# One pool of 19 slots for raw and split weight tiles, and the last tokens of a feed-forward stage ended one by one

## The chip, the core and the metric

The kernel runs on one core of a Trainium2 chip. Its engines each run their own list of instructions in order, and wait for each other by semaphores: TensorE (PE, matmuls into PSUM), VectorE (DVE), ScalarE (ACT), GpSimd (POOL) and SyncE (SP, which here only issues the DMAs). The metric is the device time of one execution in microseconds (us), lower is better.

## The reference

A decoder trunk of two layers on 512 tokens of width 1024, all in float32:

```
def reference(x, ...):
    for i in range(DEPTH):                       # 2 layers
        h = rmsnorm(x, norm_mix_pre[i])
        if i % N_MIXERS == 0:
            m = swa_sink_attention(h, ...)       # 16 heads of 64, 4 kv heads, window 128
        else:
            m = chunked_sgu(h, ...)              # gelu, layernorm, 128x128 mixing per chunk
        x = x + rmsnorm(m, norm_mix_post[i])
        h = rmsnorm(x, norm_ffn_pre[i])
        x = x + rmsnorm(swiglu(h, ffn_w_gate_up[i], ffn_w_down[i]), norm_ffn_post[i])
    return x                                     # FF = 2816
```

## The kernel before

The 512 tokens are four tiles of 128 (tokens 0 to 3 below are these tiles), 1024 is eight k-tiles of 128, and 2816 is 22. A float32 product is made of three: a value is split into a high part (`hh` for activations, `wh` for weights) and a low part (`hl`, `wl`), and `mm3` adds hh·wh, hl·wh and hh·wl in PSUM, each matmul in the helper at L272. So every weight is loaded and split before PE uses it.

Weights come in chunks of eight 128x128 blocks (128x1024 float32, 512 KB). `fetch` (L303) has SP issue the DMA into a tile `raw`; `split` has ACT copy raw to `wh` (L344), and DVE subtract, raw - wh, to `wl` (L325; POOL at L322 for the first two chunks). In parts of the feed-forward stages a chunk is the sum or difference of two raws (DVE at L337, then ACT at L332). Before, raws have a pool of their own with 4 buffers (`rawp`), and wh, wl, the gain rows and attention's values share 15 slots of 128x1024 (`wp`).

The stages are numbered 0 (Q, K, V and attention), 1 (its out-projection), 2 (first feed-forward, gate and up, and most of the down-projection), 3 (the end of its down-projection), 4 and 5 (SGU, out-projection), and 6 and 7 (second feed-forward). In stage 3 and 7 the last six k-tiles (BJ = 6) of the down-projection are added token by token and in two halves of 512 columns: the loop over `ends`. Each entry names tokens and a half; 6 k-tiles x 3 matmuls per token and half run on PE, and DVE adds the PSUM result to `m` (L901).

When both halves of a token are there, `Tok` ends it: ACT squares and sums (L476), DVE or POOL multiplies by the gain row (L604, L598), DVE computes a reciprocal root of the mean square in eight small rows (L482 and L455 to L471), and updates x in two halves (L617). When tokens 0 and 1 (or 2 and 3) are updated, `NextH` norms the pair for the next stage: the same small rows for both, a scaling (L523 on DVE, L520 on ACT), transposes on PE into `aux` (L554), and the copies `hh` (ACT, L567) and `hl` (DVE, L571) of two k-tiles at a time, which the first matmuls of the next stage read. `LastTok` is the last token of the program, cut in 256-column halves (L930, L651, L662).

In attention, ACT makes the softmax p (L1070) and scales it (L1083), PE transposes it into aux (L1116), ACT copies that to `t` (L1120), and PE multiplies t with the values vt (L1108); ACT copies the result to `ga` (L1130) and DVE makes its low part (L1135). Beside it runs the rotation of the next heads (ACT `rt`, L966; `ga<-rt`, L976).

The order of all this is set while the program is built, by a planner in the kernel: `now` is its estimate of PE's time, `busy` that of the other engines. Work beside the main matmuls is held in generators (`Side`) with due times, and `tick`, `until` and `wait` run them when they are due. `split_idle` splits the next chunk early when engines are idle or the chunk is urgent, by the numbers of `PLAN` for the stage, `pace` and `hold` (a time before which the next chunk isn't needed). `used` and `raw_used` count slots that are taken in the plan; `cur` is the chunk that PE is at. A change in any of these moves instructions on several engines.

Of the kernel before, what the change touches and what calls it, by code (L numbers as in the profile page):

```python
# [6 lines left out]
F32 = mybir.dt.float32  # L7
# [6 lines left out]
P = 128  # L14
# [7 lines left out]
CB = 8  # L22
NEG = -1.0e30
MAGIC = 0x5F3759DF
NW = 15
NP = 2
PITCH = 0.107
NY = 3
P0 = 3
NT = 3  # L30
NRAW = 4
SETS = (8, 8)
AJ = sum(SETS)
BJ = NJ - AJ
# [60 lines left out]
def _stream():  # L95

    st, n = [], [0]

    def plain(blocks, uses):
        for _ in range(blocks // CB):  # L100
            st.append(((n[0],), 0, uses))
            n[0] += 1

    def ffn():
        plain(3 * 2 * KT, 2)
        plain((SETS[0] - 3) * 2 * KT, 1)
        gb = n[0]
        qb = gb + 2 * (NJ - SETS[0])
        for kind, a, b in ITEMS:
            if kind == "g":  # L110
                st.append(((gb + 2 * (a - SETS[0]) + b,), 0, 1))
            else:
                x, y, sign = PRODUCTS[a[1]][1]
                at = lambda z: qb + 4 * b + 2 * z[0] + z[1]
                st.append(((at(x),) if y is None else (at(x), at(y)), sign, 2))
        n[0] = qb + 4 * NQ
        plain(2 * BJ * 4, 4)

    plain(16, 4)
    plain(80, 1)  # L120
    plain(64, 4)
    ffn()
    plain(32, 4)
    plain(16, 2)
    plain(32, 4)
    plain(48, 1)
    plain(64, 4)
    ffn()
    return st, n[0]


STREAM, NHBM = _stream()
# [17 lines left out]
def trunk_kernel(ctx, tc, x_t, xt, w, cols, rows, ws_t, consts, out):  # L150
    nc = tc.nc
    pool = lambda n, b, **k: ctx.enter_context(tc.tile_pool(name=n, bufs=b, **k))
# [2 lines left out]
    hp = pool("hp", KT)  # L155
    mp = pool("mp", 2 * NB)
    gp = pool("gp", 2)
    rawp = pool("rawp", NRAW)
    wp = pool("wp", NW)
    tp = pool("tp", 3)  # L160
    sp = pool("sp", 3)
# [5 lines left out]
    def nm(s):  # L167
        cnt[0] += 1
        return f"{s}_{cnt[0]}"
# [26 lines left out]
    now = [0.0]  # L196
# [23 lines left out]
    def first():  # L220
        return min(sides, key=lambda s: s.due)

    def tick():
        while True:
            if sides and first().due <= now[0]:
                first().step()
            elif not split_idle():
                return
# [21 lines left out]
    def until(f):  # L250
        while not f():
            tick()
            if not f():
                pass_time(max(now[0] + 0.01, first().due))
# [29 lines left out]
    NCH = NBLK // CB  # L284
    raws, chunks = {}, {}
    used, cur, hold, pace = [0], [0], [0.0], [5.1]
    left = [CB * u for _, _, u in STREAM]
    raw_used = [0]

    def fetch(free=0.0, most=NBLK):  # L290
        while len(raws) < min(NCH, most) and raw_used[0] + len(STREAM[len(raws)][0]) <= NRAW:
            c = len(raws)
            if c == NLATE:
                load_x()
            if c == NLATE + 1:
                nc.sync.dma_start(c_msk[:, 0:256], consts[:, 1024:1280])
                nc.sync.dma_start(c_msk[:, 256:384], consts[:, 1408:1536])
                nc.sync.dma_start(cs[:], consts[:, 0:1024])
                busy["d"] += 2.5
            tiles = []  # L300
            for b in reversed(STREAM[c][0]):
                raw = rawp.tile([P, CB * P], F32, tag="raw", name=nm("raw"))
                nc.sync.dma_start(raw[:], w[b])  # L303
                busy["d"] = max(busy["d"], now[0], free) + 1.46
                tiles.insert(0, raw)
            raw_used[0] += len(tiles)
            raws[c] = (tiles, busy["d"] + DLAT)

    def split():
        c = len(chunks)  # L310
        fetch()
        tiles, ready = raws[c]
        raw = tiles[0]
        assert used[0] + 2 <= NW
        used[0] += 2
        wh = wp.tile([P, CB * P], F32R, tag="w", name=nm("wh"))
        wl = wp.tile([P, CB * P], F32R, tag="w", name=nm("wl"))

        def low(f):
            yield f  # L320
            if c in POOL_LOW:
                nc.gpsimd.tensor_tensor(wl[:], raw[:], wh[:].bitcast(F32), ALU.subtract)  # L322
                chunks[c][3] = f + 2.4
            else:
                nc.vector.tensor_tensor(wl[:], raw[:], wh[:].bitcast(F32), ALU.subtract)  # L325
                chunks[c][3] = V(CB * P, f)
            raw_used[0] -= 1
            fetch(chunks[c][3])

        def high_low(f):  # L330
            yield f
            nc.scalar.activation(wh[:], raw[:], AF.Copy)  # L332
            yield from low(A(CB * P, f))

        if len(tiles) == 2:
            op = ALU.add if STREAM[c][1] > 0 else ALU.subtract
            nc.vector.tensor_tensor(raw[:], raw[:], tiles[1][:], op)  # L337
            f = V(CB * P, ready)
            raw_used[0] -= 1
            fetch(f)  # L340
            chunks[c] = [wh, wl, None, None, f]
            chunks[c][2] = Side(high_low(f), f)
            return
        nc.scalar.activation(wh[:], raw[:], AF.Copy)  # L344
        f = A(CB * P, ready)
        chunks[c] = [wh, wl, None, None, f]
        chunks[c][2] = Side(low(f), f)

    def split_idle():
        c = len(chunks)  # L350
        if c >= NCH or used[0] + 2 + spare[0] > NW or (c and not chunks[c - 1][2].done):
            return False
        if c not in raws or raws[c][1] > now[0]:
            return False
        slack = max(now[0], hold[0]) + (c - cur[0] - 1) * pace[0] - max(now[0], busy["v"], busy["a"]) - (2.4 if len(STREAM[c][0]) == 1 else 3.7)
        urgent, idle, ahead = PLAN[stage[0]][:3]
        if slack > urgent:
            if max(busy["v"], busy["a"]) > now[0] + idle or any(s.chain and s.due < now[0] + ahead for s in sides):
                return False
        split()  # L360
        return True

    spare, stage = [0], [0]

    def chunk(i):
        c = i // CB
        while c >= len(chunks):
            until(lambda: not chunks or chunks[len(chunks) - 1][2].done)
            split()
        return c, chunks[c]  # L370

    def high(i, n):
# [15 lines left out]
        return ch[0][:, o:o + w], ch[1][:, o:o + w]  # L388

    def row_tile(o):  # L390
        used[0] += 1
        assert used[0] <= NW
        t = wp.tile([P, D], F32, tag="w", name=nm("row"))
        nc.sync.dma_start(t[:], rows[272 + o * D:272 + (o + 1) * D].partition_broadcast(P))
        return t
# [308 lines left out]
    def ffn(base, nx_in, g1o, nx_out):  # L704
# [186 lines left out]
        d0 = at  # L891
        l = gsrc(g)
        if 1:
            spare[0] = 0
            g1 = row_tile(g1o)
            toks = [Tok(t, m[t], g1, nx_out) for t in range(NB)]
            if nx_out is None:
                toks[-1] = LastTok(NB - 1, m[-1], g1, m[0])

            def add(t, c, ps):  # L900
                nc.vector.tensor_tensor(m[t][c][:], ps[:], m[t][c][:], ALU.add)  # L901
                toks[t].add(c, ps, V(S, now[0] + 0.2))

            ends = [(0, 0), (0, 1), (1, 0), (1, 1)]
            if nx_out is None:
                ends.pop()
            ends = [((0, 1), 0), ((0, 1), 1)] + [((2 + i,), c) for i, c in ends]
            for n, (ts, c) in enumerate(ends):
                if n == 2:
                    hold[0] = now[0] + 4 * BJ * 0.65  # L910
                for t in ts:
                    grab("acc")
                ps = [acc() for _ in ts]
                for k in range(BJ):
                    for t, q in zip(ts, ps):
                        tok_mm(q, l, t, k, d0 + c * BJ * 4 + 4 * k, k == 0, k == BJ - 1)
                for t, q in zip(ts, ps):
                    add(t, c, q)
            if nx_out is None:
                t = NB - 1  # L920
                until(lambda: toks[0].done)
                for i, hf in enumerate(halves):
                    grab("acc")
                    ps = acc()[:, 0:256]
                    for k in range(BJ):
                        lh, ll = l(k, slice(t * P, (t + 1) * P))
                        wh, wl = blk(d0 + BJ * 4 + 4 * k, 4 if i else 0, 4)
                        mm3(ps, lh, ll, wh[:, hf], wl[:, hf], k == 0, k == BJ - 1)
                        tick()
                    nc.vector.tensor_tensor(m[t][1][:, hf], ps, m[t][1][:, hf], ALU.add)  # L930
                    toks[t].add(i + 1, ps, V(256, now[0] + 0.2))
            else:
                drop_after(toks)
# [613 lines left out]
```

## Time and profile before

| | before |
|---|---|
| median of 3 runs | 1058.82 us (1058.65 to 1059.26) |
| the profiled execution | 1059.33 us, span 1057.5 us |
| PE busy | 1031.1 us (97%), mean granted clock 0.989 |
| PE weight loads busy | 854.7 us (81%) |
| DVE busy | 684.7 us (65%) |
| ACT busy | 469.6 us (44%) |
| POOL busy | 23.8 us (2%) |
| raw DMAs | 240 of 512 KB, 3.6 us from issue to landing (median) |

Busy time is the time in which an engine had an instruction of its own running. In a row of a timeline the first number is the start in us from the span's start, the second the time it took (several equal rows together as xN), then engine, line, operation and output<-inputs; in brackets stands how long the engine idled before it, and the instruction that released it. In a row of a table of stretches stand the length, the busy time and count of PE, PEld, DVE, ACT and POOL, the granted clock of PE, the share of the DMA engines and GB/s. Groups by line show busy time and the mean in ns of one.

### The profile page before, as it was taken

To read this page: it belongs to the slowest core of one execution; us is meant where nothing else is said; L and a number is where in the kernel's file an instruction comes from. 1 tells how busy PE (TensorE), PEld (TensorE's weight loads), DVE (VectorE), ACT (ScalarE), POOL (GpSimd) and SP (SyncE) were. 2 spreads that over 40 slices of the span, in tenths; PEclk is the share of its full clock that TensorE was granted. 3 is DMA by queue.
4 is the path that set the end of the run, shared out by engine and by line. 5 is a ranking of instruction groups with operands and counts; after the bars stand their busy time and mean duration, and the time that the engine had idled before them with its cause. 6 is when DMAs were issued, how large, how long until landed. Compare 5 with 4: busy or idle time off the path is not lost.

```text
span 1057.5 us, 13471 instructions
## 1 busy us (share of the span) xinstructions
PE 1031.1 (97%) x5126; PEld 854.7 (81%) x5126; DVE 684.7 (65%) x1276; ACT 469.6 (44%) x817; POOL 23.8 (2%) x22
## 2 busy tenths in 40 slices
PE   8998998999999999999989999999999999999996
PEld 7875665998888888888878888899888888888885
DVE  6798678743446566778495777474245666687736
ACT  5798666542233343435265343464224333334411
POOL 2000002000000000000010000010000000000000
PEclk9998999999999999999999999999999999999999
DMA  9422011343425644655431333133344553565402
GB/s 334 138 82 80 21 60 41 100 127 113 139 82 178 199 122 157 222 188 191 156 116 60 104 103 121 56 121 120 120 140 131 178 174 124 188 203 193 163 21 80
DMA packets 39057, 138.66 MB, mean 131 GB/s; under 512 B 4368, under 2 KB 4896, under 8 KB 38992
## 3 DMA queue, kind: packets, MB, share of 16 engines
q1 hardware_dynamic: 38304, 136.66, 39.3%
q8 instruction: 40, 0.66, 0.3%
q10 hardware_dynamic: 576, 0.92, 0.2%
q0 software_dynamic: 112, 0.23, 0.2%
q14 instruction: 25, 0.20, 0.1%
HBM read 135.69 MB, written 2.10 MB: 130 GB/s over the span
## 4 chain that ended last, share of the span: by engine, by line
PE 92%; DVE 3%; ACT 2%; issue 1%; DMA 0%; POOL 0%; DVEq 0%; ACTq 0%; POOLq 0%
PE acc L272 89%; PE acc L1108 1%; PE aux L1116 1%; PE aux L554 1%; ACT p L1070 1%; DMA c_cols<-cols 0%; ACT rt L966 0%; DVE wl L325 0%; DVE x L617 0%; DVE hl L1393 0%; ACT wh L344 0%; PE aux L552 0%; ACT t L1120 0%; DVE m L1210 0%; DVE rc L471 0%
## 5 line engine op out<-in xcount | busy, mean ns | idle before, releaser
L272 PE MATMUL acc<-hh,wh 128*128 128x512 f32 (+1 forms) x960 | 352.1, 367 | 0.0
L272 PE MATMUL acc<-hl,wh 128*128 128x512 f32 (+1 forms) x960 | 349.9, 364 | 0.0
L272 PE MATMUL acc<-hh,wl 128*128 128x512 f32 (+1 forms) x960 | 349.7, 364 | 0.0
L325 DVE TENSOR_TENSOR wl<-raw,wh 128x1024 fp32r<-128x1024 f32 x198 | 241.9, 1230 | 151.1 <-PE acc L272 78.2
L272 PEld LDWEIGHTS acc<-hh,wh 128*128 128x128 f32 x960 | 181.1, 189 | 29.4 <-issue 0.2
L272 PEld LDWEIGHTS acc<-hh,wl 128*128 128x128 f32 x960 | 181.1, 189 | 28.7
L272 PEld LDWEIGHTS acc<-hl,wh 128*128 128x128 f32 x960 | 181.1, 189 | 28.6 <-issue 0.2
L344 ACT ACTIVATE wh<-raw 128x1024 fp32r<-128x1024 f32 x160 | 165.6, 1052 | 55.0 <-PE acc L272 48.3
L272 PE MATMUL acc<-wh,rt 128*128 128x512 f32 x496 | 162.3, 389 | 0.0
L272 PE MATMUL acc<-wh,ga 128*128 128x512 f32 (+1 forms) x344 | 120.3, 399 | 3.6 <-DVE ga L1135 2.9
L272 PEld LDWEIGHTS acc<-wh,rt 128*128 128x128 f32 x496 | 93.1, 188 | 19.4
L272 PE MATMUL acc<-wl,rt 128*128 128x512 f32 x248 | 96.5, 389 | 0.0
L272 PEld LDWEIGHTS acc<-wh,ga 128*128 128x128 f32 x344 | 65.2, 191 | 21.1 <-DVE ga L1135 3.8
L853 DVE TENSOR_TENSOR m<-m,acc 128x512 f32<-128x512 f32 x80 | 51.8, 684 | 44.2 <-PE acc L272 33.0
L272 PE MATMUL acc<-wl,ga 128*128 128x512 f32 (+1 forms) x206 | 80.0, 388 | 0.0
L332 ACT ACTIVATE wh<-raw 128x1024 fp32r<-128x1024 f32 x40 | 42.3, 1059 | 71.0 <-DVE raw L337 71.0
L831 ACT ACTIVATE rt<-t 128x512 fp32r<-128x512 f32 x40 | 25.3, 633 | 87.1 <-DVE t L826 68.7
L740 ACT ACTIVATE t<-acc 128x512 f32<-128x512 f32 (+1 forms) x38 | 20.1, 529 | 95.0 <-PE acc L272 95.0
L272 PEld LDWEIGHTS acc<-wl,rt 128*128 128x128 f32 x248 | 46.6, 188 | 9.6
L337 DVE TENSOR_TENSOR raw<-raw,raw 128x1024 f32<-128x1024 f32 x40 | 48.8, 1219 | 0.0
L272 PEld LDWEIGHTS acc<-wl,ga 128*128 128x128 f32 x206 | 39.3, 191 | 6.6
L598 POOL TENSOR_TENSOR m<-m,row 128x512 f32<-128x512 f32 x12 | 16.8, 1407 | 1012.1 <-ACT acc L476 1012.1
(135 smaller groups left out, 990.5 us busy)
## 6 DMA issues: line engine op xcount, KB each, us to landing
raw<-w SPq DMA_DIRECT2D x240, 512.0 KB, 3.6
row<-rows SPq DMA_DIRECT2D x8, 512.0 KB, 5.2
xg<-xt SPq DMA_DIRECT2D x4, 512.0 KB, 7.1
x<-x_t SPq DMA_DIRECT2D x4, 512.0 KB, 11.9
out<-x SPq DMA_DIRECT2D x4, 256.0 KB, 2.1
out<-x ACTq DMA_DIRECT2D x3, 256.0 KB, 2.1
cs<-consts SPq DMA_DIRECT2D x1, 512.0 KB, 8.3
t<-ws_t SPq DMA_DIRECT2D x2, 256.0 KB, 5.9
```

Of the source, the lines that this page charges most:

```text
L272: nc.tensor.matmul(ps, a, b, start=start, stop=stop)
L325: nc.vector.tensor_tensor(wl[:], raw[:], wh[:].bitcast(F32), ALU.subtract)
L332: nc.scalar.activation(wh[:], raw[:], AF.Copy)
L337: nc.vector.tensor_tensor(raw[:], raw[:], tiles[1][:], op)
L344: nc.scalar.activation(wh[:], raw[:], AF.Copy)
L554: nc.tensor.transpose(dst, self.src[t][k // 4][:, (k % 4) * P:(k % 4 + 1) * P], ident)
L598: nc.gpsimd.tensor_tensor(self.m[c][:], self.m[c][:], self.g1[:, cols2[c]], ALU.mult)
L740: nc.scalar.activation(t1[:, hf], pg[:, hf], AF.Silu)
L831: nc.scalar.activation(hi, src, AF.Copy)
L853: nc.vector.tensor_tensor(d, d, ps[i][:], ALU.subtract if sign == "-" else ALU.add)
L1070: nc.scalar.activation(p(j), p(j), AF.Exp, bias=st[:, j:j + 1], accum_out=sm[:, j:j + 1])
L1108: nc.tensor.matmul(po[i * 64:i * 64 + 64, :], vt[n - nkt + 1 + kt][:, o:o + 64], todo[2 * kt + i], start=kt == 0, stop=kt == nkt - 1)
```

## The change

There is one pool of 19 slots now, for raw, wh, wl and rows. At most 4 raws are held in stages 2 and 6 and at most 2 elsewhere, and a raw, a split, or a row is planned only when the sum of all taken slots stays within 19. `row_tile` waits for a slot in the plan where it asserted one; `chunk` waits until the raw is there and two slots are free (`room`); `split` calls `fetch` no more. The variable `spare`, always 0, is gone. In `ends`, tokens 0 and 1 still take their first half together, but end the second one after the other; `hold` counts five entries instead of four.

```
-NW = 15
+NW = 19
-NRAW = 4
+NRAW = (2, 4)
...
-    rawp = pool("rawp", NRAW)
...
+    stage = [0]
     def fetch(free=0.0, most=NBLK):
-        while len(raws) < min(NCH, most) and raw_used[0] + len(STREAM[len(raws)][0]) <= NRAW:
+        while len(raws) < min(NCH, most):
             c = len(raws)
+            n = len(STREAM[c][0])
+            if raw_used[0] + n > NRAW[stage[0] in (2, 6)] or used[0] + raw_used[0] + n > NW:
+                return
...
-                raw = rawp.tile([P, CB * P], F32, tag="raw", name=nm("raw"))
+                raw = wp.tile([P, CB * P], F32, tag="w", name=nm("raw"))
...
     def split():
         c = len(chunks)
-        fetch()
         tiles, ready = raws[c]
         raw = tiles[0]
-        assert used[0] + 2 <= NW
+        assert used[0] + raw_used[0] + 2 <= NW
...
     def split_idle():
         c = len(chunks)
-        if c >= NCH or used[0] + 2 + spare[0] > NW or (c and not chunks[c - 1][2].done):
+        if c >= NCH or used[0] + raw_used[0] + 2 > NW or (c and not chunks[c - 1][2].done):
             return False
...
-    spare, stage = [0], [0]
+    def room():
+        fetch()
+        return len(chunks) in raws and used[0] + raw_used[0] + 2 <= NW

     def chunk(i):
         c = i // CB
         while c >= len(chunks):
-            until(lambda: not chunks or chunks[len(chunks) - 1][2].done)
-            split()
+            until(lambda: c < len(chunks) or (not chunks or chunks[len(chunks) - 1][2].done) and room())
+            if c >= len(chunks):
+                split()
...
     def row_tile(o):
+        until(lambda: used[0] + raw_used[0] < NW)
         used[0] += 1
-        assert used[0] <= NW
...
-            ends = [(0, 0), (0, 1), (1, 0), (1, 1)]
+            ends = [((0, 1), 0), ((0,), 1), ((1,), 1), ((2,), 0), ((2,), 1), ((3,), 0), ((3,), 1)]
             if nx_out is None:
                 ends.pop()
-            ends = [((0, 1), 0), ((0, 1), 1)] + [((2 + i,), c) for i, c in ends]
             for n, (ts, c) in enumerate(ends):
                 if n == 2:
-                    hold[0] = now[0] + 4 * BJ * 0.65
+                    hold[0] = now[0] + 5 * BJ * 0.65
```

In the rows that follow, the first word is the line, which is 4 to 6 higher in the changed kernel from `split` on, and the numbers behind names differ between the two programs for the same tile.

On DVE, at the end of the first feed-forward stage (stage 3), before: m_2822 and m_2823 are the halves of token 0, m_2824 and m_2825 those of token 1, u the start of token 0's root.

```order
L901 TENSOR_TENSOR m_2822<-acc_4485,m_2822 128x512
L901 TENSOR_TENSOR m_2824<-acc_4486,m_2824 128x512
L604 TENSOR_TENSOR m_2822<-m_2822,row_4479 128x512
L604 TENSOR_TENSOR m_2824<-m_2824,row_4479 128x512
L901 TENSOR_TENSOR m_2823<-acc_4528,m_2823 128x512
L901 TENSOR_TENSOR m_2825<-acc_4529,m_2825 128x512
L604 TENSOR_TENSOR m_2823<-m_2823,row_4479 128x512
L604 TENSOR_TENSOR m_2825<-m_2825,row_4479 128x512
L482 SCALAR_TENSOR_TENSOR u_4589<-sq_4481 128x1
```

The same place after: m_2828 and m_2829 are token 0, m_2830 and m_2831 token 1.

```order
L906 TENSOR_TENSOR m_2828<-acc_4482,m_2828 128x512
L906 TENSOR_TENSOR m_2830<-acc_4483,m_2830 128x512
L610 TENSOR_TENSOR m_2828<-m_2828,row_4476 128x512
L610 TENSOR_TENSOR m_2830<-m_2830,row_4476 128x512
L906 TENSOR_TENSOR m_2829<-acc_4523,m_2829 128x512
L610 TENSOR_TENSOR m_2829<-m_2829,row_4476 128x512
L488 SCALAR_TENSOR_TENSOR u_4559<-sq_4478 128x1
```

Token 1's second add and gain no longer stand ahead of token 0's root; they come behind token 0's update of x. The transposes of the pair (four rows of aux) and the matmuls around them on PE move too: before they stand in the second half of token 3 (acc_4717), after in its first half (acc_4687).

On ACT, in attention, before: aux_1057 is a transposed p, and PE's next matmul with the values waits for t_1062.

```order
L976 ACTIVATE ga_117<-rt_830 128x512
L1083 ACTIVATE p_863<-p_863,sm_862 128x256
L344 ACTIVATE wh_1038<-raw_757 128x1024
L966 ACTIVATE rt_1010<-rt_1010,c_cols 32x512 x4
L1083 ACTIVATE p_863<-p_863,sm_862 128x256
L1120 ACTIVATE t_1062<-aux_1057 128x512
L976 ACTIVATE ga_117<-rt_915 128x512
```

After, where that copy is t_1039 and the chunk's high part wh_1042:

```order
L980 ACTIVATE ga_114<-rt_823 128x512
L970 ACTIVATE rt_905<-rt_905,c_cols 32x512 x4
L1124 ACTIVATE t_1001<-aux_996 128x512
L1087 ACTIVATE p_853<-p_853,sm_852 128x256
L1124 ACTIVATE t_1039<-aux_1034 128x512
L1087 ACTIVATE p_853<-p_853,sm_852 128x256
L346 ACTIVATE wh_1042<-raw_936 128x1024
L970 ACTIVATE rt_1003<-rt_1003,c_cols 32x512 x4
L1134 ACTIVATE ga_114<-acc_967 128x4x128
```

The copy stands ahead of the chunk's high part and of the four rt now; the four rt of the heads before (rt_905) have moved in front of the copy t_1001.

Some heads later on ACT, before:

```order
L1083 ACTIVATE p_1461<-p_1461,sm_1460 128x256
L1067 ACTIVATE es_1459<-es_1459 128x4
L1070 ACTIVATE p_1461,sm_1460<-p_1461,st_1458 128x256 x4
L476 ACTIVATE acc_1500,sq_1499<-m_1011 128x512
L344 ACTIVATE wh_1584<-raw_997 128x1024
L1120 ACTIVATE t_1592<-aux_1587 128x512
```

and after:

```order
L1087 ACTIVATE p_1454<-p_1454,sm_1453 128x256
L1071 ACTIVATE es_1452<-es_1452 128x4
L1074 ACTIVATE p_1454,sm_1453<-p_1454,st_1451 128x256 x4
L1124 ACTIVATE t_1577<-aux_1572 128x512
L482 ACTIVATE acc_1493,sq_1492<-m_1004 128x512
L346 ACTIVATE wh_1584<-raw_1264 128x1024
```

The copy t has passed a square (L476, now L482) and the high part of a chunk.

More of the change, by code (lines that the diff above doesn't have):

```diff
@@ L893, in ffn @@
         if 1:
-            spare[0] = 0
             g1 = row_tile(g1o)
```

## The prediction

> **What bounds the kernel now.** I read the chain that ended last first, then the waits of TensorE (PE), then a table of stretches by time, and last the timelines of the engines around each wait.
>
> ```profile
> PE 92%; DVE 3%; ACT 2%; issue 1%; DMA 0%; POOL 0%; DVEq 0%; ACTq 0%; POOLq 0%
> ...
> PE acc L1108 <- ACT t L1120: 6.6, 3, 3.8
> ...
> PE acc L272 <- DVE ga L1135: 2.9, 2, 2.6
> PE acc L272 <- DVE hl L571: 2.7, 1, 2.7
> ...
> PE acc L272 <- DVE hl L1393: 0.8, 1, 0.8
> ...
> 92.00:106.00 14.00, 9.94 (x39) 4.84 (x38) 10.28 (x26) 10.23 (x18) 0.00 (x0) 0.76 0.23 75
> ...
> 146.00:156.00 10.00, 7.42 (x35) 4.24 (x34) 6.11 (x20) 6.67 (x19) 0.00 (x0) 0.84 0.16 51
> ...
> 176.00:187.00 11.00, 7.71 (x24) 4.59 (x23) 10.74 (x36) 5.96 (x14) 2.80 (x2) 0.84 0.30 96
> 187.00:512.00 325.00, 325.00 (x1596) 275.96 (x1595) 198.56 (x266) 125.98 (x173) 0.00 (x0) 1.00 0.48 156
> ...
> 548.00:556.00 8.00, 5.32 (x18) 3.81 (x17) 7.91 (x14) 4.66 (x11) 0.00 (x0) 0.79 0.83 294
> ```
>
> The chain is PE for 92%: the kernel is bound by its matmuls, whose number the change leaves alone. From 187 to 512 us (the first feed-forward stage) PE is busy for all 325.00 us at full clock: there is nothing to gain there, however early weights come. What can be gained is PE's waits and the slow clock behind them. The waits that this change can touch are three in attention (two for ACT's copy t, up to 3.8 us, one for DVE's ga, 2.6) and one of 2.7 us for DVE's hl, where the first feed-forward stage hands over to the SGU. In each of the four stretches with such a wait the granted clock (the last column but two) falls below 1. Length times missing clock, 14 x 0.24 = 3.4, 10 x 0.16 = 1.6, 11 x 0.16 = 1.8 and 8 x 0.21 = 1.7 us, bounds from above what the slow clock costs there; part of it falls into the waits themselves.
>
> **The change, part by part.** No instruction is added and none goes; what changes is who waits behind whom.
>
> *The end of the first feed-forward stage.* PE's rows at the hand-over:
>
> ```profile
> 547.77 0.40 PE L272 MATMUL acc<-wh,hh 128*128 128x512 f32 x1
> 548.00 0.39 PE L272 MATMUL acc<-wl,hh 128*128 128x512 f32 x1
> 551.07 0.50 PE L272 MATMUL acc<-wh,hl 128*128 128x512 f32 x1 [2.68 <-DVE hl L571]
> ...
> 553.65 0.63 PE L272 MATMUL acc<-wl,hh 128*128 128x512 f32 x1
> 554.07 0.63 PE L272 MATMUL acc<-wh,hl 128*128 128x512 f32 x1
> ```
>
> A matmul starts every 0.23 us before the wait and every 0.42 after it; the wait costs 2.7 us and the slow clock behind it up to the 1.7 above, 4.4 together. DVE before it:
>
> ```profile
> 528.20 1.37 DVE L901 TENSOR_TENSOR m<-acc,m 128x512 f32<-128x512 f32 x2 [5.30 <-PE acc L272]
> ...
> 534.74 1.41 DVE L617 SCALAR_TENSOR_TENSOR x<-m,rc,x 128x512 f32<-128x512 f32 x2
> ...
> 537.04 0.69 DVE L901 TENSOR_TENSOR m<-acc,m 128x512 f32<-128x512 f32 x1 [0.29 <-PE acc L272]
> ...
> 540.18 0.89 DVE L523 TENSOR_SCALAR m<-x,rc 128x512 f32<-128x512 f32 x2
> 541.12 0.69 DVE L901 TENSOR_TENSOR m<-acc,m 128x512 f32<-128x512 f32 x1
> ...
> 549.40 1.21 DVE L325 TENSOR_TENSOR wl<-raw,wh 128x1024 fp32r<-128x1024 f32 x1
> 550.54 0.87 DVE L571 SCALAR_TENSOR_TENSOR hl<-aux,c_cols,hh 128x256 fp32r<-128x256 f32 x2
> ```
>
> One token's half takes PE 541.12 - 537.04 = 4.08 us. Before, tokens 0 and 1 end their second half together, so DVE idles for 5.30 us up to 528.20 and then has both tokens' adds, gains, norms and updates in one pile, the last ended at 536.15; the norm of the pair and the scaling follow (540.18), then the transposes on PE and the hl that PE waits for (550.54), which by then stands behind token 2's update and wl of chunk 88. After, token 0 ends 4.08 us earlier, at about 524.6, and its gain, norm and update (some 4 us: add 0.69, a gain of as much, the small rows of the norm 1.2, the update 1.41) fit into the idle 5.30 us. Token 1's add is at 528.7, and what was two tokens' work behind it is one's: its update ends near 532.7 instead of 536.15, and the scaling comes some 3.2 us earlier. The transposes stand three chunks earlier in PE's order, so the hl of k-tiles 2 and 3 falls near 546.5 (estimate, from these rows shifted), ahead of PE's need at 548.4. Late next are wl of chunk 89 (about 550.5, needed about 550.3) and hl 4, 5 (548.6, needed 548.9): I leave 0.3 us of wait. **Term: -4.1**, between -4.4 and 0 (if the next wait takes all of it).
>
> *Attention, order alone.* The shared pool lets the planner split a chunk at other moments, and ACT's and DVE's rows move past each other. First wait, ACT:
>
> ```profile
> 94.04 0.49 ACT L1083 ACTIVATE p<-p,sm 128x256 f32<-128x256 f32 x1
> 94.44 1.04 ACT L344 ACTIVATE wh<-raw 128x1024 fp32r<-128x1024 f32 x1
> 95.51 2.91 ACT L966 ACTIVATE rt<-rt,c_cols 32x512 f32<-32x512 f32 x4
> ...
> 98.86 0.58 ACT L1120 ACTIVATE t<-aux 128x512 f32<-128x512 f32 x1
> ```
>
> The copy t for which PE stands still reads the transposes of an earlier p, but stands behind wh of chunk 16 and four rt, 1.04 + 2.91 us, and a second p. In the new order it comes ahead of these; the earlier four rt now stand ahead of the t before it. ACT would then end the two copies near 94.5 and 95.4, and PE, which has six matmuls moved up between, would be there near 92.9: waits of about 1.6 + 0.4 instead of 3.8 + 0.3, -2.1. What it passes, wh and rt, is due later: PE's next copy then falls near 100.2, as PE comes for it. Second wait:
>
> ```profile
> 149.61 0.58 ACT L476 ACTIVATE acc<-m 128x512 f32<-128x512 f32 x1
> ...
> 150.22 1.04 ACT L344 ACTIVATE wh<-raw 128x1024 fp32r<-128x1024 f32 x1
> 151.17 0.57 ACT L1120 ACTIVATE t<-aux 128x512 f32<-128x512 f32 x1
> ```
>
> PE waits 2.6 us for this t (the three waits of the row above are 6.6 in all, the largest 3.8 and a small one 0.3). It now goes ahead of a square and wh of chunk 19: 151.17 - 149.61 = 1.56 us earlier on ACT, and six matmuls move ahead of PE's wait, which cover some of it but come out of its later cover: -1.4. Third wait, DVE:
>
> ```profile
> 178.07 2.43 DVE L617 SCALAR_TENSOR_TENSOR x<-m,rc,x 128x512 f32<-128x512 f32 x2
> 180.42 1.21 DVE L325 TENSOR_TENSOR wl<-raw,wh 128x1024 fp32r<-128x1024 f32 x1
> 181.56 0.68 DVE L1210 TENSOR_TENSOR m<-acc,m 128x512 f32<-128x512 f32 x1
> 182.16 0.68 DVE L1135 TENSOR_TENSOR ga<-acc,ga 128x512 fp32r<-128x512 f32 x1
> ```
>
> The ga goes ahead of an m (0.6 us on DVE), and six matmuls (6 x 0.23 = 1.4 us) move in front of PE's wait of 2.6: -1.8. Together -5.3. Of this I give 2.0 back to waits that come next: 0.9 where PE needs p scaled for the next transposes in the second place, 0.7 at the third, 0.4 at the first. The slow clock of these three places costs at most 3.4 + 1.6 + 1.8 = 6.8 us; I take 2.0, since waits of 1 to 2 us remain, and no wait of that length stands in an attention row of before. **Term: -5.3**, between -12.1 (all waits and all slow clock) and +2 (new waits as large as the old and one more slow stretch).
>
> On the slow clock, the page "TensorE: Matmul & The Clock Gate" of the Trainium skill (section "What's actually happening") says that the clock is halved after an idle window of about 3.4 us, which runs free of the program. By it only the wait of 3.8 us would be certain to be followed by a slow stretch, and the 1.7 us at the hand-over would not hang on its wait; the sum by it would be 1.4 us smaller there. The trace differs: the wait of 2.68 us above is followed by matmuls at 0.42 us.
>
> *The end.* DVE's rows, and PE's last:
>
> ```profile
> 1049.30 0.28 PE L272 MATMUL acc<-wh,gb 128*128 128x256 f32 x1
> ...
> 1048.75 1.41 DVE L617 SCALAR_TENSOR_TENSOR x<-m,rc,x 128x512 f32<-128x512 f32 x2
> 1050.08 0.75 DVE L930 TENSOR_TENSOR m<-acc,m 128x256 f32<-128x256 f32 x2
> ...
> 1051.68 0.16 DVE L482 SCALAR_TENSOR_TENSOR u<-sq 128x1 f32<-128x1 f32 x1
> ```
>
> The same split of tokens 0 and 1 stands in the last stage. Before, token 2's update holds DVE until 1050.16, while PE's last matmul ends at 1049.6; the two adds of token 3 wait. After, the update stands ahead of token 3's work, and the last add can start with PE's end: add and gain of 0.37 each and a square of 0.58 on ACT give a u near 1050.75. **Term: -0.9**, between -1.1 and 0.
>
> *At nothing.* Raws come from the 19 slots. From the fifth on they no longer wait at the head for the reader of an earlier raw, and so land earlier, while PE still waits for ACT and for data that stand ahead of them in the same SP queue. The limit of two raws outside stages 2 and 6 is covered by this group's price and the chunk's time:
>
> ```profile
> L325 DVE TENSOR_TENSOR wl<-raw,wh 128x1024 fp32r<-128x1024 f32 x198 | 241.9, 1230 | 151.1 <-PE acc L272 78.2
> ...
> L332 ACT ACTIVATE wh<-raw 128x1024 fp32r<-128x1024 f32 x40 | 42.3, 1059 | 71.0 <-DVE raw L337 71.0
> ...
> raw<-w SPq DMA_DIRECT2D x240, 512.0 KB, 3.6
> ```
>
> From issue to usable a chunk takes 3.6 + 1.06 + 1.23 = 5.9 us, and 1.2 more for a pair (7.1); a chunk lasts PE 1057.5 / 200 = 5.3 us on the mean, so two chunks ahead (10.6 us) suffice. On SP a row now goes ahead of raw 18, 21 and 110 and three rows ahead of raw 91, and a ws_t goes behind raw 89; each of these raws is one to three transfers later (raw 91 waits for its slot anyway). A waiting raw holds every DMA behind it: raw 90 now waits for a slot until about 540.6 (it was issued at 516.4 before), raw 91 and 92 until 545.4 and 546.9; landing takes 3.6, and PE comes to chunk 90 at about 557. The wait of row_tile falls where slots are free, and the hold of 5 instead of 4 halves shifts only the planner's clock. If that cover goes, the price is that of the last rival.
>
> **The sum.** -4.1 - 5.3 - 0.9 = -10.3, from the profiled execution's 1059.33 (span 1057.5): 1049.0. That execution lies 0.5 above the median of the runs shown, so the forecast on the median is **1048.5**.
>
> **Rivals.** *Only the ends gain.* In attention ACT's work is the same and only queues up elsewhere: ACT was 10.23 of 14 us busy at the first wait, so wh and rt put back could become the next wait of the same length. For it: the window's row; against it: ACT's slack behind. It gives 1058.8 - 5.0 = 1053.8.
>
> *All goes and nothing comes back.* 4.4 + 5.3 + 6.8 + 0.9 = 17.4 less: 1041.4. Against it: three places have to fall below the wait that slows the clock, which lies between the 0.8 us of hl L1393, with matmuls at full speed behind it, and 2.6.
>
> *Shorter waits slow the clock all the same.* The waits of 1 to 2 us that I leave in attention are spread over more places; were each still followed by a stretch like 1.6 to 3.4, the clock would give nothing and PE would save 3.3 there: 1058.8 - 4.1 - 3.3 - 0.9 = 1050.5. The same page of the Trainium skill (section "A second HAM failure mode: psum-queue depth-cycling") tells of such short idling that keeps the clock swinging; no run here shows it yet.
>
> *Nothing is gained.* Chunk 87 can't be split before a slot pair comes free, in either order; if its wl now stops DVE ahead of the hl, the 2.7 us of the hand-over come back under another name, and with attention as in the first rival only the end is left: 1057.9.
>
> *Slower.* A raw that waits for the last matmul on a slot blocks SP's queue, and the chunks behind are late. A pair takes 7.1 us from issue, a chunk lasts 5.3, so a pair issued one chunk ahead is 1.8 us late. Ten of the 40 pairs late give 18 us: 1048.5 + 18 = 1066.5. It decides from seven pairs (12.4 us, the gain and the 0.2%). Against it: stages 2 and 6 keep four raws and thus the 15 slots they had.
>
> **How the numbers follow.** Forecast 0.45, with the clock rival (0.10) inside its own range 1045.5 to 1052; ends alone 0.20; all goes 0.10; nothing 0.08; slower 0.07. What a measurement tells from no change is 0.2%, 2.1 us (1056.7 to 1060.9). The range goes from 1043.5 to 1056.5: it takes in the forecast, the clock rival, most of the ends alone and the near side of "all goes". Faster 0.85, same 0.08, slower 0.07.
>
> **What would show it.** In the profile of the changed kernel: the wait for hl L571 (now L577) gone or under 1 us and a clock of 1.00 from 548 to 556; token 0's update done before token 1's add; waits for t under 2 us at the two places in attention, with a clock above 0.9 in the first stretch; the last u<-sq 1.2 us after PE's last matmul instead of 2.1. Wrong would be: waits of PE for wl or wh in stages 2 or 6, SP's raws issued behind PE's need, or a new wait of over 2.5 us between 95 and 187.

## The result, and the profile after

The changed kernel takes 1044.41 us (median of 4, 1042.74 to 1044.54), against 1059.04 for the kernel before: a ratio of 0.9858, with a 95% interval of 0.9841 to 0.9875. That is 14.6 us less; the forecast was 1048.5, 10.3 less, with a range of 1043.5 to 1056.5 that holds the result. The profiled execution took 1044.39 us, its span is 1042.6.

The waits of PE in the changed kernel (total, times, longest, in us; the lines of the two programs differ by a few, L271 is L272 of before, L346 is L344, L1124 is L1120):

```profile
PE aux L1120 <- ACT t L1124: 3.6, 3, 2.4
PE acc L271 <- ACT wh L346: 3.1, 1, 3.1
PE acc L271 <- DVE ga L1139: 2.7, 1, 2.7
```

Gone are the three waits for t ahead of the matmuls with the values (6.6 us) and the one for hl at the hand-over (2.7); the wait for wh at the start, 3.1, is as it was. PE's transposes wait for t now, 3.6 us in three waits where it was one of 0.5, and one wait for ga is left. The table of stretches (length, busy time and count of PE, PEld, DVE, ACT, POOL, granted clock, DMA share, GB/s) has the rest:

```profile
92.00:106.00 14.00, 11.61 (x66) 6.65 (x63) 13.14 (x38) 12.63 (x28) 0.00 (x0) 0.88 0.11 37
146.00:156.00 10.00, 9.75 (x61) 5.49 (x60) 8.71 (x34) 7.74 (x21) 0.00 (x0) 1.00 0.00 0
156.00:176.00 20.00, 17.34 (x77) 12.34 (x77) 17.53 (x47) 14.19 (x38) 4.98 (x4) 0.93 0.09 27
176.00:187.00 11.00, 11.00 (x76) 10.13 (x76) 10.62 (x30) 7.59 (x20) 0.51 (x1) 0.97 0.64 208
187.00:503.00 316.00, 316.00 (x1528) 267.45 (x1527) 190.42 (x247) 118.86 (x157) 0.00 (x0) 1.00 0.47 155
...
537.00:556.00 19.00, 19.00 (x115) 16.83 (x114) 15.53 (x45) 11.89 (x24) 0.00 (x0) 1.00 0.44 162
```

PE works through the hand-over (537 to 556) without a gap at full clock. To see where the gain comes from, I compare when PE reaches the same chunk in the two traces, here chunk 20 and chunk 90 before, and then after:

```profile
191.43 0.28 PE L272 MATMUL acc<-hh,wh 128*128 128x256 f32 x1
...
562.50 0.28 PE L272 MATMUL acc<-hh,wh 128*128 128x256 f32 x1
```

```profile
182.13 0.28 PE L271 MATMUL acc<-hh,wh 128*128 128x256 f32 x1
...
548.49 0.28 PE L271 MATMUL acc<-hh,wh 128*128 128x256 f32 x1
```

Chunk 20, which opens the first feed-forward stage, is reached at 191.43 before and 182.13 after (9.3 us gained by then); chunk 80, where that stage's end begins, at 512.36 and 503.08 (still 9.3); chunk 90, in the SGU, at 562.50 and 548.49 (14.0); PE's last matmul ends at 1049.58 and 1035.65 (13.9). Between these two executions, 14.9 us apart, attention thus gave 9.3, the hand-over 4.7, the end 1.0, and the two long feed-forward stages nothing.

### The profile page after: what moved, and what is told of

Read it like the earlier page. It is cut to its first block, busy times and chain, and to the rows that moved or that the text cites. A ratio compares the mean times of both kernels' runs of the same rounds, so it can differ in the third digit from the quotient of the medians.

```text
span 1042.6 us, 13488 instructions
## 1 busy us (share of the span) xinstructions
PE 1024.4 (98%) x5126; PEld 850.9 (82%) x5126; DVE 683.8 (66%) x1276; ACT 470.0 (45%) x817; POOL 23.9 (2%) x22
## 4 chain that ended last, share of the span: by engine, by line
PE 88%; ACT 5%; DVE 5%; issue 1%; DMA 1%; POOL 0%; DVEq 0%; ACTq 0%; POOLq 0%
PE acc L271 85%; ACT rt L970 2%; ACT p L1074 1%; ACT wh L346 1%; DVE wl L327 1%; PE aux L560 1%; DVE p L1052 1%; PE acc L1112 1%; DMA c_cols<-cols 1%; DVE p L1083 0%; PE aux L1120 0%; ACT t L1124 0%; DVE hl L1397 0%; PE aux L558 0%; ACT p L1087 0%
## 5 line engine op out<-in xcount | busy, mean ns | idle before, releaser
L271 PE MATMUL acc<-hh,wh 128*128 128x512 f32 (+1 forms) x960 | 352.0, 367 | 0.0
L271 PE MATMUL acc<-hl,wh 128*128 128x512 f32 (+1 forms) x960 | 349.8, 364 | 0.0
L271 PE MATMUL acc<-hh,wl 128*128 128x512 f32 (+1 forms) x960 | 349.7, 364 | 0.0
L271 PEld LDWEIGHTS acc<-hh,wh 128*128 128x128 f32 x960 | 181.1, 189 | 29.5 <-issue 0.2
L271 PEld LDWEIGHTS acc<-hl,wh 128*128 128x128 f32 x960 | 181.1, 189 | 28.6 <-issue 0.2
L271 PEld LDWEIGHTS acc<-hh,wl 128*128 128x128 f32 x960 | 181.1, 189 | 28.6
L346 ACT ACTIVATE wh<-raw 128x1024 fp32r<-128x1024 f32 x160 | 165.8, 1052 | 83.9 <-PE acc L271 57.6
L271 PE MATMUL acc<-wh,rt 128*128 128x512 f32 x496 | 162.3, 389 | 0.0
L271 PE MATMUL acc<-wh,ga 128*128 128x512 f32 (+1 forms) x344 | 119.8, 398 | 2.7 <-DVE ga L1139 2.7
L271 PEld LDWEIGHTS acc<-wh,rt 128*128 128x128 f32 x496 | 93.1, 188 | 19.4
L271 PE MATMUL acc<-wl,rt 128*128 128x512 f32 x248 | 96.5, 389 | 0.0
L271 PEld LDWEIGHTS acc<-wh,ga 128*128 128x128 f32 x344 | 65.0, 190 | 20.4 <-issue 4.9
L271 PE MATMUL acc<-wl,ga 128*128 128x512 f32 (+1 forms) x206 | 79.5, 386 | 0.0
L271 PEld LDWEIGHTS acc<-wl,rt 128*128 128x128 f32 x248 | 46.6, 188 | 9.6
L271 PEld LDWEIGHTS acc<-wl,ga 128*128 128x128 f32 x206 | 39.1, 190 | 6.5
```

The lines of the kernel that those rows point to most:

```text
L271: nc.tensor.matmul(ps, a, b, start=start, stop=stop)
```

## The experiments

Each was timed beside the kernel before, on the same chip.

**The new ends alone** (pools as before):

```
-            ends = [(0, 0), (0, 1), (1, 0), (1, 1)]
+            ends = [((0, 1), 0), ((0,), 1), ((1,), 1), ((2,), 0), ((2,), 1), ((3,), 0), ((3,), 1)]
...
-            ends = [((0, 1), 0), ((0, 1), 1)] + [((2 + i,), c) for i, c in ends]
...
-                    hold[0] = now[0] + 4 * BJ * 0.65
+                    hold[0] = now[0] + 5 * BJ * 0.65
```

> Before, with the new order of the ends alone (pools and raw limits as before). Theory (two separate gains): the order of attention is that of before, so the waits of 3.8, 2.6 and 2.6 us stay; the wait for hl at the hand-over to the SGU goes and the end is 1 us shorter: 4.7 + 1.0 less than before, about 1053.3. Rival (the hand-over gains by the shared pool, which splits chunks 87 and 88 at other moments): the wait for hl stays over 2 us, only the end gains, about 1058.

Measured: 1053.81 us against 1059.05, ratio 0.9954 (0.9939 to 0.9969). The waits of attention are those of before, the wait for hl is gone:

```profile
PE acc L1107 <- ACT t L1119: 6.6, 3, 3.8
...
PE acc L272 <- DVE ga L1134: 2.9, 2, 2.6
```

So hand-over and end are the work of the order of the ends, 5.2 us together, but for 0.4: from chunk 80 to chunk 90 PE takes 45.82 us here, 50.14 before and 45.41 in the changed kernel. The 0.4 left is a short stop ahead of a matmul with hl (0.51 us between two starts, at 552.28, in place of 0.23).

**The pool alone** (old ends):

```
-            ends = [((0, 1), 0), ((0,), 1), ((1,), 1), ((2,), 0), ((2,), 1), ((3,), 0), ((3,), 1)]
+            ends = [(0, 0), (0, 1), (1, 0), (1, 1)]
...
+            ends = [((0, 1), 0), ((0, 1), 1)] + [((2 + i,), c) for i, c in ends]
...
-                    hold[0] = now[0] + 5 * BJ * 0.65
+                    hold[0] = now[0] + 4 * BJ * 0.65
```

> The changed kernel with the ends in the order of before. Theory: attention as in the changed kernel, so the first feed-forward stage starts 9.3 us earlier than before; the wait for hl of 2.7 us with its slow clock stays: about 1049.7. Rival (the shared pool brings the hand-over too): the wait for hl is gone, about 1045.

Measured: 1048.89, ratio 0.9905 (0.9889 to 0.9922). The wait for hl is back at 2.7. The two parts are independent as far as the intervals tell (each some 1.7 us to either side): 5.2 and 10.2 against 14.6 together. This run holds a second finding. Its rows in attention are the very rows of the changed kernel, and so are its waits (3.5 us for t, 2.7 for ga), but not its clock:

```profile
92.00:106.00 14.00, 11.61 (x72) 7.03 (x71) 13.13 (x38) 13.45 (x28) 0.00 (x0) 1.00 0.12 39
...
156.00:176.00 20.00, 17.20 (x81) 11.99 (x79) 17.72 (x52) 13.04 (x33) 5.51 (x4) 1.00 0.14 46
176.00:187.00 11.00, 10.31 (x78) 9.67 (x79) 10.78 (x26) 8.94 (x20) 0.00 (x0) 1.00 0.62 205
```

The clock stayed at 1.00 behind waits of 2.4 and 2.7 us, where the changed kernel's profile has 0.88, 0.93 and 0.97, and PE came to chunk 20 at 179.90 instead of 182.13. A wait of that length is followed by the slow clock in some executions and not in others; what decides it is told under "The clock" below.

**Two pools, but at most 2 raws outside stages 2 and 6** (old ends, 4 + 15 slots):

```
+NLIM = (2, 4)
...
-        while ... raw_used[0] + len(STREAM[len(raws)][0]) <= NRAW:
+        while ... raw_used[0] + len(STREAM[len(raws)][0]) <= NLIM[stage[0] in (2, 6)]:
```

> Before with two pools (4 + 15), old ends, but the planner holds at most 2 raws outside stages 2 and 6. Theory (the limit in the plan alone moves attention's rows): the first wait for t, 3.8 us, becomes two smaller ones as in the changed kernel, since ACT's first 130 rows are the same; later rows of attention differ, so between 2.5 and 9 us less: 1050 to 1056.5. Rival (what counts is where raws lie and when they land): as before, 1059.

Measured: 1055.68, ratio 0.9969 (0.9958 to 0.9981). The wait of 3.8 became one of 2.4 ahead of the transposes, the other two stayed at 2.6 each:

```profile
PE aux L1118 <- ACT t L1122: 3.8, 3, 2.4
...
PE acc L273 <- DVE ga L1137: 3.0, 2, 2.6
...
PE acc L1110 <- ACT t L1122: 2.6, 1, 2.6
```

The limit in the plan moves the first place; the second moves in the next run, which has the slots that the limit frees.

**Two pools of 2 raws and 17 slots, everywhere** (old ends):

```
-NW = 15
+NW = 17
...
-NRAW = 4
+NRAW = 2
```

> Two pools of 2 raws and 17 other slots everywhere, old ends: no slot is shared, but through attention PE, ACT and DVE have the very rows of the changed kernel. Theory (the gain in attention is the order, not the sharing): the first feed-forward stage starts 9.3 us earlier than before, and the three waits there are those of the changed kernel (2.4, 0.9, 2.7). Beyond that 2 raws serve the feed-forward stages, where pairs take both: with no new wait about 1049.7; if a pair is late by 1.8 us in ten places, 1068. Rival (sharing lets raws land earlier): attention gains less than 5 us.

Measured: 1114.33, ratio 1.0533 (1.0512 to 1.0554). Chunk 20 is reached at 182.11, 9.3 us before the kernel before, with not one shared slot: attention's gain is the order that the plan makes from its counts. The time is far over both forecasts, 1049.7 and 1068. PE takes 33.8 us longer than before from chunk 20 to 80 and 32.6 longer from chunk 90 to its end, the stretches with the two feed-forward stages, and waits there at the pairs:

```profile
PE acc L272 <- ACT wh L332: 19.9, 15, 3.1
PE acc L272 <- DVE wl L325: 13.9, 22, 0.8
```

Two raws can't hold the next pair while one is being read. These two waits are half of the loss; the other half, with ten stretches of 3.4 us at half clock and the restarts behind the waits in it, I did not split up. My last rival, pairs that come late, is thus real, but only where raws are few in stages 2 and 6.

**One pool, new ends, 4 raws in every stage:**

```
-NRAW = (2, 4)
+NRAW = (4, 4)
```

> The changed kernel, but with up to 4 raws planned in every stage, so 15 slots for all else everywhere: one shared pool and the new ends. Through attention PE, ACT and DVE then have the rows of before. Theory (sharing by itself gives nothing, the limit of 2 raws gives attention's gain): as with the new ends alone, 1053.8, with waits of 3.8, 2.6 and 2.6. Rival (raws that land earlier help by themselves): 1051 or less.

Measured: 1053.24, ratio 0.9949 (0.9937 to 0.9962), as with the ends alone, and with the old waits in attention:

```profile
PE acc L1112 <- ACT t L1124: 6.6, 3, 3.8
...
PE acc L271 <- DVE ga L1139: 3.0, 2, 2.6
```

From chunk 80 to 90 PE takes 45.85 us, as with the ends alone, so the 0.4 us there, too, come with the limit of 2 raws and not with the sharing. Sharing slots gives nothing by itself here. It gives the freedom to hold 2 raws and 17 others in one stage, and 4 and 15 in another, in the same memory.

**20 transposes to fill a wait**, first put at the wrong unit:

```
+                if (pr, n, z) == (0, 3, 2):
+                    for q in range(20):
+                        nc.tensor.transpose(po[:, 0:P], u.pt[:, 0, 0, 0:P], ident)
                 pT = aux()
```

> The changed kernel, with 20 transposes into a PSUM tile that isn't used yet, put on PE ahead of the transposes that wait 2.4 us at 98.0 for a copy t. They fill the wait and compute nothing that is used. Theory (an idle PE loses its clock): the wait falls under 0.5 us and the clock from 92 to 106, 0.88 in the changed kernel, is 1.00, so 14 x 0.12 = 1.7 us less than the changed kernel where that one fell into the slow stretch: about 1042.7. Rival (the clock falls for another reason than this wait): 0.88 stays, 1044.4.

Measured: 1045.92, ratio 0.9879 (0.9864 to 0.9893). They came to stand at 119, far from the wait, which stayed at 2.4; they took 2.35 us of PE's time and say nothing on the theory. Put one unit earlier, `(0, 2, 2)`:

> The changed kernel with the 20 transposes now one unit of attention earlier, so that they stand on PE at 98.0, right ahead of the transposes that wait 2.4 us for a copy t (the first try put them at 119, beside no wait, where they cost 2.35 us). They take about 2.3 us at full clock. Theory (an idle PE loses its clock): the wait falls under 0.5 us and the clock from 88 to 106 is 1.00 in the profile, so up to 1.7 us less than the changed kernel: 1042.7. Rival (the clock falls for another reason): below 0.95 as in the changed kernel, 1044.4 or more.

Measured: 1043.05, ratio 0.9852 (0.9837 to 0.9867). PE's timeline, and the stretch around it:

```profile
98.14 2.35 PE L1120 MATMUL acc<-c_id,p 128*128 128x128 f32 x20
100.71 0.66 PE L1123 MATMUL aux<-c_id,p 128*128 128x128 f32 x4 [0.22 <-ACT t L1127]
```

```profile
92.00:106.00 14.00, 13.78 (x93) 9.16 (x91) 13.14 (x38) 13.15 (x28) 0.00 (x0) 1.00 0.13 39
```

The data comes no earlier, but the clock is 1.00 now, and PE comes to chunk 16 at 135.97 instead of 137.52: 1.5 us, against 1.7 forecast. The pool-alone run has 1.00 here without a filling, so this profile by itself doesn't prove it; the size is near that of the lost clock, 14 x 0.12, and PE's idle time, 0.22 us in place of 2.39, is by "The clock" below too little for a slow stretch wherever it falls.

**Chunk 16 split later:**

```
+        if c == 16 and cur[0] < 14:
+            return False
```

> The changed kernel, but chunk 16 isn't split before PE has come to chunk 14, so that its wh (1.05 us on ACT) no longer stands ahead of the copy t at 100.0. PE wants chunk 16 at 137.5. Theory (ACT's queue makes the wait of 2.4 us): it falls to about 1.3, 1.0 to 2.7 us less than the changed kernel with the slow clock: 1041.7 to 1043.4. Rival (the plan shifts other rows of attention, and the same work waits elsewhere): 1044 or more.

Measured: 1045.70, ratio 0.9876 (0.986 to 0.9893). The wait at 98 fell from 2.4 to 1.4, as ACT's queue says:

```profile
99.55 0.66 PE L1122 MATMUL aux<-c_id,p 128*128 128x128 f32 x4 [1.44 <-ACT t L1126]
```

But new waits for t (1.9 in two ahead of matmuls, 0.6 ahead of transposes) and one of 0.7 for ga came in its place, the old one for ga stayed (2.6), and chunk 20 was reached at 182.28, as in the changed kernel, though the clock was 1.00 all through attention. The mechanism holds, the gain doesn't: the rival was right about the time.

**The wl of chunk 21 later:**

```
-            yield f
+            yield f + (3.0 if c == 21 else 0.0)
```

> The changed kernel, with wl of chunk 21 held back by 3 us in the plan, so that on DVE it stands behind ga and m instead of ahead of them. PE wants chunk 21 at 186.8. Theory (the wl, 2.29 us, makes PE's wait for ga of 2.7 us at 171): the wait falls to about 0.4 and the slow clock behind it goes: 2.3 to 4.0 us less than the changed kernel, 1040.4 to 1042.1. Rival (ga waits for x's update and the result of PE, wl only stands beside it): 1044.4.

Measured: 1043.22, ratio 0.9851 (0.9837 to 0.9866). PE's wait for ga fell from 2.7 to 0.4 and the clock behind it is 1.00, so chunk 20 is reached 2.4 us earlier (179.70). Then PE waits 2.1 us for hl, and at chunk 22 it is at 189.82, 0.2 us behind the changed kernel:

```profile
182.12 0.38 PE L271 MATMUL acc<-hl,wh 128*128 128x256 f32 x1 [2.06 <-DVE hl L577]
```

The same work of DVE stood in front of the next thing that PE wants: DVE starts that hl at 181.59, and at 181.58 in the changed kernel. The profile shows less than the edit is worth, though. In this execution the slow clock behind the wait at 98 lasted twice as long (two windows, 0.79 from 92 to 106, against 0.88), so PE came 1.1 us later to the ga, and DVE to the rows before the hl. The time is above the forecast of 1040.4 to 1042.1.

**Token 2's gains on DVE instead of POOL:**

```
-... (6.0, 0.8, 0.0, (3,), (1, 2)) ...
+... (6.0, 0.8, 0.0, (3,), (1,)) ...
```

> The changed kernel, with token 2's two gains of stage 1 on DVE (0.7 us each) instead of POOL; one of them then stands between wl of chunk 21 and ga. Theory (a DVE row that runs beside POOL's gain is slowed by it: 2.29 us for that wl, 1.21 elsewhere): the wl takes 1.21 again, PE's wait for ga falls from 2.7 to 2.3: about 1044.0. Rival (the wl is slow for another reason): 2.29 stays, the wait grows to 3.4: about 1045.1.

Measured: 1043.57, ratio 0.9857 (0.9842 to 0.9871). DVE in the changed kernel, with POOL's row beside it, and then DVE in this run:

```profile
170.89 2.29 DVE L327 TENSOR_TENSOR wl<-raw,wh 128x1024 fp32r<-128x1024 f32 x1
173.10 0.68 DVE L1139 TENSOR_TENSOR ga<-acc,ga 128x512 fp32r<-128x512 f32 x1
```

```profile
170.50 1.60 POOL L604 TENSOR_TENSOR m<-m,row 128x512 f32<-128x512 f32 x1 [2.10 <-ACT acc L482]
```

```profile
171.59 1.22 DVE L327 TENSOR_TENSOR wl<-raw,wh 128x1024 fp32r<-128x1024 f32 x1
172.72 0.69 DVE L610 TENSOR_TENSOR m<-m,row 128x512 f32<-128x512 f32 x1
173.32 0.68 DVE L1139 TENSOR_TENSOR ga<-acc,ga 128x512 fp32r<-128x512 f32 x1
```

Without POOL's gain beside it the wl takes 1.22, and PE's wait is 2.2 in place of 2.7 (2.3 expected), although DVE has a row more ahead of ga. In time that is too little to be seen.

**Filling and late wl together:**

> Both the 20 transposes at 98 and the late wl of chunk 21, as a try for a faster version. Theory: the clock is 1.00 through attention, what is left are waits: 1041.5 to 1043. Rival: 1044, as the changed kernel.

Measured: 1043.16, ratio 0.9849 (0.9835 to 0.9862). In its profile the clock is 1.00 from 88 to 187 and PE is at chunk 22 2.4 us ahead of the changed kernel, and at chunk 80 (500.64) 1.1 us ahead of the run with the filling alone (501.76). In time the three variants (0.9849 to 0.9852) can't be told from the changed kernel (0.9858): the intervals lie on each other. None is a proven better kernel.

## Why the prediction was right, and where its sizes were off

All three places gained, two of them much as forecast, and the total gain came out 4.3 us larger than forecast: 1044.4 lies below the 1045.5 to 1052 to which I had given the most, near "all goes". Of my signs, those of the hand-over and of the end came. Two in attention did not: a wait for t was 2.4 us where I had put under 2, and the clock of the first stretch 0.88 where I had put over 0.9. The wait of 2.7 us for ga at 171 is even over the 2.5 that I had called wrong for a new wait, though one of 2.6 stood there before.

**The hand-over: right, -4.1 forecast, -4.7 measured.** DVE's rows after:

```profile
518.88 1.41 DVE L623 SCALAR_TENSOR_TENSOR x<-m,rc,x 128x512 f32<-128x512 f32 x2
520.21 0.68 DVE L906 TENSOR_TENSOR m<-acc,m 128x512 f32<-128x512 f32 x1
...
528.17 0.88 DVE L529 TENSOR_SCALAR m<-x,rc 128x512 f32<-128x512 f32 x2
...
536.32 0.87 DVE L577 SCALAR_TENSOR_TENSOR hl<-aux,c_cols,hh 128x256 fp32r<-128x256 f32 x2
```

Token 0's update now stands ahead of token 1's second add. Read with attention's 9.3 us added, the scaling is at 537.5 and the hl at 545.6, where 540.18 and 550.54 stood before. The scaling is 2.7 us earlier (some 3.2 were forecast), and the hl falls a little before the 546.5 forecast. The leftover wait that I allowed for did not come. The run with the ends alone shows that the order of the ends gives 4.3 of the 4.7. That the gain passed my bound of 4.4 has a reason: I had priced the wait by PE's idle time, 2.68 us, but from the last matmul before it (548.00) to the second start after it (551.55) PE took 3.55 us for two steps of 0.23, so the wait with its restart cost 3.1.

**The end: right, -0.9 forecast, -1.0 measured.** In the changed kernel the last root starts 1.1 us after PE's end at 1035.65, and not 2.1:

```profile
1035.69 0.42 DVE L934 TENSOR_TENSOR m<-acc,m 128x256 f32<-128x256 f32 x1 [0.73 <-PE acc L271]
...
1036.75 0.16 DVE L488 SCALAR_TENSOR_TENSOR u<-sq 128x1 f32<-128x1 f32 x1 [0.18 <-ACT acc L655]
```

**Attention: right way, mis-sized, -5.3 forecast, -9.3 measured.** The waits there were 10.7 us before (6.6 for t, 2.9 and 0.7 for ga, 0.5 for the transposes) and are 6.3 after (3.6 and 2.7): -4.4, where the term had -5.3 + 2.0 = -3.3. The other 4.9 us are the time behind the waits, for which I had put 2.0. By the stretches the slow clock cost at most 6.8 us before and 14 x 0.12 + 20 x 0.07 + 11 x 0.03 = 3.4 after. The gain from it, 3.4 at most, came at two places: the second lost its wait, 2.6 us becoming 0.25, and with it the whole slow stretch, and the first lost half of its own. Of this half, and of any slow stretch, a part is luck: the pool-alone run, with the same rows of attention, had none. The restart behind a wait is a term that I put at nothing; at the hand-over it was 0.4 us, and attention has three waits fewer, so I estimate 1.2 for it. So the term was too small in its waits (by 1.1), in its clock (by 1.4 at most) and in the restart, and some 0.3 us or more stay open.

By places, three steps came out otherwise than written. At the first I had PE meet its next copy at 100.2 without a wait. ACT's timeline and PE's row say why it waited 2.4:

```profile
95.52 1.05 ACT L346 ACTIVATE wh<-raw 128x1024 fp32r<-128x1024 f32 x1
96.59 2.91 ACT L970 ACTIVATE rt<-rt,c_cols 32x512 f32<-32x512 f32 x4
99.53 0.60 ACT L1134 ACTIVATE ga<-acc 128x512 fp32r<-128x512 f32 x1
100.03 0.59 ACT L1124 ACTIVATE t<-aux 128x512 f32<-128x512 f32 x1
```

```profile
100.67 0.66 PE L1120 MATMUL aux<-c_id,p 128*128 128x128 f32 x4 [2.39 <-ACT t L1124]
```

The copy ends at 100.62, about where I had it; but there are two aux buffers, and PE's third set of transposes needs the first one copied out. The wh and the rt that the copy had passed stand before the next copy, so 3.8 us became 2.4 (and 0.9 for the pair before). That is the first rival's mechanism, for a part of the wait. The later split of chunk 16 confirms it: without the 1.05 us of wh the wait is 1.4.

At the second place the wait fell from 2.6 to 0.25 (1.4 gained was forecast, 2.3 came), and the clock there rose from 0.84 to 1.00:

```profile
149.78 0.66 PE L1120 MATMUL aux<-c_id,p 128*128 128x128 f32 x4 [0.25 <-ACT t L1124]
```

At the third I forecast a gain of 1.8 in the wait for ga; it is 2.7, where it was 2.6. The wl ahead of ga took 2.29 us beside POOL's gain, 1.07 more than alone, which took back what the passed m had given (0.6). What came instead were the small waits for ga and the transposes before it (0.7, 0.5 and a few tenths), which are gone.

**The clock.** My sentence that waits of 2.6 us are followed by the slow clock was true of the kernel before, and not a rule: the pool-alone run has the same waits at full clock. The clock records of the traces show what decides it. In all 13 traces the clock keeps its value for windows of 3.413 us, one behind the other, and where the borders fall differs from execution to execution. The windows around the same wait of 2.39 us, first in the changed kernel and then in the pool-alone run (columns as in the tables of stretches):

```profile
98.26:101.67 3.41, 1.02 (x11) 0.83 (x12) 3.34 (x11) 3.35 (x7) 0.00 (x0) 1.00 0.00 0
101.67:105.08 3.41, 3.41 (x17) 1.58 (x14) 3.31 (x13) 2.63 (x11) 0.00 (x0) 0.50 0.00 0
```

```profile
96.14:99.56 3.42, 2.47 (x22) 1.63 (x20) 3.35 (x12) 3.36 (x5) 0.00 (x0) 1.00 0.00 0
99.56:102.97 3.41, 1.97 (x19) 1.38 (x20) 3.34 (x7) 3.36 (x9) 0.00 (x0) 1.00 0.00 0
102.97:106.38 3.41, 3.41 (x19) 2.20 (x17) 3.31 (x14) 2.66 (x10) 0.00 (x0) 1.00 0.00 0
```

In the changed kernel one window holds the whole wait, and the next has half the clock. In the other execution a border parts the wait, PE idles for 0.95 and 1.44 us of two windows, and the clock stays. From 20 us to PE's end, the traces together have 3847 windows at full clock: none of the 3809 in which PE idled for less than 1.6 us was followed by one at half clock, all of the 25 with 1.95 or more were, and of the 13 between 9 were. (The ends of matmuls are modelled, so the idle times are rough.) So not the length of a wait alone decides, as I had it in the rivals, but how much idle time falls into one window. The Trainium skill ("TensorE: Matmul & The Clock Gate", section "What's actually happening") tells of a free-running window of 3413 ns, and the traces agree with that. That such a window has to be idle throughout, as I had read it, they do not show: even the wait of 3.8 us in the kernel before lay in two windows, with 2.42 and 1.36 us. By that reading the sum would also have been 1.7 us smaller at the hand-over, not 1.4.

**At nothing: right.** The two long feed-forward stages gained and lost nothing (9.3 us at chunk 20 and at chunk 80, 14.0 at chunk 90 and 13.9 at PE's end), and no row moved on SP made anything late.

## What to carry to other kernels

The pool shared by two kinds of tiles was worth no time by itself here; its worth was what the counts let the planner do in each stage, so look for the stage in which the old split was the wrong one, and test it with the counts alone. When two units end at the same moment and the engine that finishes them sat idle just before, let them end one after the other. Before you book a wait as gone, follow the work that was passed to the next thing in its queue: here most of what one row gave, the next row that PE wanted took back. And a wait needn't be gone to cost no clock: here it was enough that less than 1.6 us of idle time fell into one window of 3.4.

## What the runs showed that I had not expected

A row on DVE with two inputs in SBUF stands still while POOL runs a multiplication of its own: the wl that started at 170.89 ended at 173.18, 1.08 us after POOL's row (170.50 + 1.60 = 172.10), and takes 1.22 when POOL is idle. The Trainium skill says this of the shared port pair ("SBUF — State Buffer", section "SBUF: two separate sides": an exclusive lock, the loser waits for the whole instruction), and the trace agrees with it. In the kernel before the same can be read from the two halves of an update that took 2.43 us at 178.07, beside a row of POOL from 178.43 to 179.95, and 1.41 elsewhere.

The same program differs by some 1.8 us from one execution to the next (1042.74 to 1044.54, with a mean clock of 0.997 in the shortest and 0.994 in the others). A window at half clock takes 3.413 x 0.5 / 1042.6 = 0.0016 off the mean clock, so the shortest execution had some two of them fewer; only one execution was traced, so where is not shown. It limits what can be told apart here.
